# Experts in fp32 on unsplit weights, in groups of 32 slots over four column tiles, with empty groups left out on PE

## The chip, the cores and the metric

One core of a Trainium2 chip runs the whole program in one launch. The metric is the device time of one execution in microseconds. PE multiplies matrices, DVE, ACT and POOL work on vectors, SP issues loads; each runs its own queue of instructions in order. Products land in PSUM, a memory of eight banks of 128 partitions x 512 fp32 values.

## The reference

Two layers act on 256 latent and 256 context tokens of 1024 features. Layer 0 has a recurrent mixer (RG-LRU) and a dense SwiGLU, layer 1 has neighbourhood attention and, for the latent tokens alone, a mixture of eight experts. The change is in the experts:

```python
D_MODEL, SEQ, D_FF, N_EXPERTS, TOP_K = 1024, 256, 3584, 8, 2

def swiglu(z, w_gu, w_down):
    g, u = jnp.split(z @ w_gu, 2, axis=-1)
    return (jax.nn.silu(g) * u) @ w_down

def moe_swiglu(z, router, w_gu, w_down):
    logits = (z @ router).astype(jnp.float32)
    top_v, top_i = lax.top_k(logits, TOP_K)
    wts = jax.nn.softmax(top_v, axis=-1)
    gates = jnp.sum(jax.nn.one_hot(top_i, N_EXPERTS, dtype=jnp.float32) * wts[..., None], axis=-2)
    out = jnp.zeros_like(z)
    for e in range(N_EXPERTS):
        out = out + gates[..., e:e + 1].astype(z.dtype) * swiglu(z, w_gu[e], w_down[e])
    return out
```

All weights are fp32. The experts' are 8 x (1024 x 7168 + 3584 x 1024) values, 352 MB. On the reference's own inputs the router sends 19, 86, 51, 92, 45, 74, 37 and 108 of the 512 choices to experts 0 to 7.

## The kernel before

The program works through layer 0, attention, the output projection with the router, and then the experts, all on one core. Almost every product is made of float32r products: `mm3` (lines 297 to 301) splits both operands into a high and a low part and sums high x high, high x low and low x high, 128 x 128 stationary by up to 512 columns moving.

An expert's weights are cut into 1 MB tiles of 128 partitions x 2048 values: 28 tiles `m_up` (gate and up columns of 512 hidden features, four tiles for each of seven chunks) and 14 tiles `m_down` (two for each chunk), 336 tiles for eight experts. `plan2` lists them in the order of their use. The class `Halves` (lines 200 to 248) moves them. `load` (line 208) takes a free buffer and has SP issue the load (line 212) as long as there are free buffers. `split` (line 216) takes half of a tile: ACT copies it to the high part `whi` (line 224), and DVE, or every 13th time POOL, writes the rest `wlo` (line 229). After the second half the 1 MB buffer is free and the next load may start. `M.ahead` lets four halves be split ahead of their use. There are 17 buffers of 1 MB for the experts: five of their own (`NR`) and those that the weights of the earlier stages give back at the end of the output projection.

An expert has 128 slots. `onehots` (line 1291) compares a token's position in the expert with the slot numbers, `gather` (line 1300) multiplies the turned tokens by these and gives the expert's tokens `xghi`, `xglo`, features on partitions. `up_chunk` (line 1339) multiplies the tokens as stationary operand by the 512 gate and the 512 up columns of a chunk, 48 products, into the banks `pg` and `pu`; then silu, a product, and `turn` (line 1358), four transposes, whose result is split again. `down_chunk` (line 1373) adds 24 products to the two banks `py`. All 128 slots are computed, however many are filled: 72 products for a chunk, 4032 for the eight experts. `gated` (line 1416) scales by the gate, and `combine` (line 1425) brings the slots back to the tokens with the turned one-hots `oht` and adds to `xl`. The loop at line 1472 runs eight experts x seven chunks; a chunk's down products are behind the up products of the next chunk, and the gather of the next expert is at the end of chunk 6. Small steps stand between the up tiles (`between`). What follows a product on ACT or DVE is held in `late` and written behind the next split, so that the splits come first on these engines. The experts stand under a manual schedule: the order of the program is that of the code.

At the end (line 1516) each engine reads the largest number of an expert's tokens and branches past a loop (line 1517) that handles more than 128 tokens.

Of the kernel before, what the change touches and what calls it, by code (L numbers as in the profile page):

```python
# [35 lines left out]
NCOL = C_LT + 64  # L36

# The steps of the mixer in the order of the program: what, which tile, on which engines.
# [16 lines left out]
# The steps of a head in attention, and how many heads ahead of the values.  # L55
# [3 lines left out]
# Buffers, and how far the experts' splits run ahead: in general and in the last chunk and the last products.  # L59
NW, NH, NL = 7, 5, 5  # L60
AHEAD, AH6, AHL, THIRD = 4, 3, 2, 13
NU, NM, NR, LEAD = 45, 8, 5, 3
# [18 lines left out]
class Weights:  # L81
    """The weights in the order of their use: a load starts as soon as a buffer is free, splits run `split` tiles ahead."""
# [45 lines left out]
    def in_two(self, how=None, lazy=False):  # L128
        """The high part of the next tile; the low one with the call of what it returns."""
# [45 lines left out]
    def get(self, key):  # L175
        """The next tile; it is used up before the next call, if it isn't split."""
# [23 lines left out]
class Halves:  # L200
    """The experts' weights, split by half tiles, `ahead` of them ahead: a load starts as soon as a buffer is free."""

    def __init__(self, nc, free, plan, q, hi=None, lo=None, ahead=1):
        self.nc, self.free, self.plan, self.q, self.hi, self.lo, self.ahead = nc, list(free), plan, q, hi, lo, ahead
        self.i = self.dma = self.spl = self.third = 0
        self.t, self.parts = {}, {}
# [9 lines left out]
    def split(self):  # L216
        """The high part of the next half; the low one with the call of what it returns."""
        self.load()
        i, h = divmod(self.spl, 2)
        assert i < self.dma  # L220
        r, pool = self.t[i]
        s = r[:, h * D:(h + 1) * D]
        hi, lo = (p.tile([P, D], F32R, name=n, tag="w") for p, n in ((self.hi, "whi"), (self.lo, "wlo")))
        self.nc.scalar.activation(hi, s, AF.Copy)  # L224
        eng = self.nc.gpsimd if self.third and self.spl % self.third == 0 else self.nc.vector
        self.spl += 1

        def rest():
            eng.tensor_tensor(lo, s, hi.bitcast(F32), op=OP.subtract)  # L229
            self.parts[2 * i + h] = hi, lo  # L230
            if h:
                del self.t[i]
                self.free.append(pool)
                self.load()

        return rest

    def ready(self):
        while self.spl < min(self.i + self.ahead, 2 * len(self.plan)):
            self.split()()  # L240

    def get(self, key):
        assert self.plan[self.i // 2][0] == key
        self.i += 1
        self.ready()
        if self.spl < self.i:
            self.split()()
        return self.parts.pop(self.i - 1)


def build(tc, a, out):
# [5 lines left out]
    with tc.tile_pool(name="k", bufs=1) as kp, \  # L257
# [112 lines left out]
        for e in range(NE):  # L370
            for c in range(7):
                for i in range(4):
                    plan2.append(("mup", a["m_up"][e, 4 * c + i]))
                if e or c:
                    for i in range(2):
                        plan2.append(("mdown", a["m_down"][e if c else e - 1, 2 * ((c - 1) % 7) + i]))
        for i in range(2):
            plan2.append(("mdown", a["m_down"][NE - 1, 12 + i]))
        M = Halves(nc, [], plan2, nc.sync)
# [3 lines left out]
        # ---- constants and inputs  # L383
# [27 lines left out]
        def warm(n):  # L411
            """Products of zeros: the tensor engine's clock is up only after a while of work."""
# [8 lines left out]
        def ada_dve(raw, l, c, f, vs):  # L421
            """One tile of 128 columns of the modulation: a product and a sum over k."""
# [15 lines left out]
        # ---- RMS norms: sums of squares with the tokens on partitions, the factors turned back  # L438
        class Norm:
            """`vs` are the context's and the latent tokens (0 and 1) or one of the two."""  # L440
# [44 lines left out]
            def start(self, k, xk, vs=None):  # L485
                """h = x * rstd * A + B, as its float32r part and, with end, the rest."""
# [77 lines left out]
        # ---- layer 0: the first norm and its modulation, in two halves of the features  # L564
# [7 lines left out]
        def ada_first(k):  # L572
            """Shift and scale of 128 features, with a sum over four parts of k left."""
# [17 lines left out]
        # ---- RG-LRU: input branch, with k outside so that the products follow the modulation  # L591
# [43 lines left out]
        def two_parts(name, src, how):  # L635
            """The float32r part of a tile and the rest; `how` has the engines."""
# [12 lines left out]
        def do_in(f, how):  # L649
            """The last two tiles of the input branch."""  # L650
# [9 lines left out]
        def do_decay(n, how):  # L660
            """softplus(-lam) as max(-lam, 0) + log1p(exp(-|lam|)), the last by its atanh series."""
# [31 lines left out]
        def do_gz(f, how):  # L693
            """A tile of the gate branch."""
# [14 lines left out]
        def do_gate(i, how):  # L709
            """The two gates of a tile and a direction."""  # L710
# [18 lines left out]
        def do_coef(i, how):  # L729
            """a and 1 - a^2; 1 - a = -expm1(log a) = tanh(-log a / 2) (1 + exp(log a))."""  # L730
# [48 lines left out]
        def do_ada(i, how):  # L779
            """A tile of the modulations of the first residual and of the second norm; the last four have two rows of tiles."""  # L780
# [29 lines left out]
        def do_po(k, how):  # L810
            """What a tile of y adds to the first columns of the output projection."""
# [69 lines left out]
        # ---- SwiGLU of layer 0  # L881
# [71 lines left out]
        # ---- neighbourhood attention of layer 1: keys, queries and their norms  # L953
# [17 lines left out]
        def head_sums(f, x, ps, n):  # L971
            """The sums of squares of the tile's two heads, on the heads' partitions."""
# [74 lines left out]
        # ---- attention, a pipeline over the heads; queries on partitions in the scores  # L1047
# [141 lines left out]
        M.hi, M.lo = (stack.enter_context(tc.tile_pool(name=n, bufs=b)) for n, b in (("mhi", NH), ("mlo", NL)))  # L1189
        M.ahead, M.third = AHEAD, THIRD  # L1190
# [4 lines left out]
        # ---- output projection; the router and the turned tokens take x * A before the norm's factor and shift  # L1195
# [86 lines left out]
        def flush():  # L1282
            while late:
                late.pop(0)()
# [397 lines left out]
```

## Time and profile before

| | |
|---|---|
| median of two runs | 1972.46 us (1970.64 to 1974.28) |
| the profiled execution | span 1972.6 us |
| PE busy | 1912.1 us (97%) |
| DVE, ACT, POOL busy | 1548.6, 1204.5, 326.4 us |
| DMA, mean over the span | 250 GB/s |
| experts' tiles loaded | 336 of 1 MB |

A row of a group gives the line, the engine, the operation, what it writes and reads, how often it ran, its busy time and the mean of one. Ends of products are modelled from their starts, so products that follow each other overlap in the rows: the distance of two starts is what one costs. The 40 slices of the page are 49.3 us each.

### The profile page before, as it was taken

What the parts mean: (1) busy time and instruction counts of PE and PEld (TensorE: products, weight loads), DVE (VectorE), ACT (ScalarE), POOL (GpSimd) and SP (SyncE); (2) the same over time, 40 slices, a digit from 0 to 9 for tenths busy, and PEclk for the clock granted to TensorE, in tenths of its full rate; (3) what the DMA queues carried; (4) which work ended last, traced back from release to release, by engine and by line L of the source; (5) the groups of instructions that cost most, each with busy time, mean ns of one, the idle gap of its engine ahead of it and who ended that gap; (6) DMA issues with size and microseconds to landing.
All of it is one profiled execution on the core that took longest, in us unless ns stands there. A gap on an engine that the chain in (4) does not pass through costs nothing.

```text
span 1972.6 us, 25338 instructions
## 1 busy us (share of the span) xinstructions
PE 1912.1 (97%) x9467; PEld 1592.9 (81%) x9467; DVE 1548.6 (79%) x2023; ACT 1204.5 (61%) x1488; POOL 326.4 (17%) x218
## 2 busy tenths in 40 slices
PE   9995899999999999999999999999999999999998
PEld 7773688888888888878888888888888888888886
DVE  4799868767454663558798998999989999899997
ACT  4576443222222235457688788787887877878785
POOL 0277600000000012325011110101111011111110
PEclk8997899999999999999999999999999999999999
DMA  9462225435353552321899999999999999999990
GB/s 360 149 235 113 92 85 175 175 130 203 128 183 130 184 184 86 127 76 60 345 366 375 343 361 349 355 372 342 361 358 355 364 340 364 350 357 365 346 351 23
DMA packets 76019, 493.97 MB, mean 250 GB/s; under 512 B 8560, under 2 KB 9600, under 8 KB 20336
## 3 DMA queue, kind: packets, MB, share of 16 engines
q1 hardware_dynamic: 74592, 487.62, 66.4%
q0 software_dynamic: 1296, 4.65, 0.7%
q8 instruction: 76, 1.25, 0.3%
q14 instruction: 55, 0.45, 0.1%
HBM read 491.19 MB, written 1.05 MB: 250 GB/s over the span
## 4 chain that ended last, share of the span: by engine, by line
PE 54%; DVE 2%; issue 0%; ACT 0%; POOL 0%; DVEq 0%; POOLq 0%; ACTq 0%
PE pg L299 5%; PE py L299 5%; PE pg L301 5%; PE pu L299 5%; PE pg L300 5%; PE pu L301 5%; PE pu L300 5%; PE py L301 5%; PE py L300 5%; PE pgx L1305 2%; PE pt L1362 1%; PE ptt L1110 0%; PE po L299 0%; PE po L300 0%; PE po L301 0%; DVE ps L1086 0%
## 5 line engine op out<-in xcount | busy, mean ns | idle before, releaser
L229 DVE TENSOR_TENSOR wlo<-raw,whi 128x1024 fp32r<-128x1024 f32 x620 | 784.9, 1300 | 75.9 <-ACT whi L224 58.8
L224 ACT ACTIVATE whi<-raw 128x1024 fp32r<-128x1024 f32 x672 | 712.9, 1062 | 187.1 <-PE pu L301 136.6
L145 ACT ACTIVATE whi<-raw 128x2048 fp32r<-128x2048 f32 (+2 forms) x72 | 125.6, 1748 | 263.2 <-PE pu L300 116.5
L229 POOL TENSOR_TENSOR wlo<-raw,whi 128x1024 fp32r<-128x1024 f32 x52 | 130.0, 2500 | 885.9 <-ACT whi L224 849.2
L151 DVE TENSOR_TENSOR wlo<-raw,whi 128x2048 fp32r<-128x2048 f32 (+2 forms) x75 | 161.2, 2153 | 82.2 <-ACT whi L145 72.6
L299 PE MATMUL pg<-whi,xghi 128*128 128x512 f32 x448 | 179.3, 400 | 0.0
L299 PE MATMUL py<-whi,mhi 128*128 128x512 f32 x448 | 175.8, 392 | 0.0
L299 PE MATMUL pu<-whi,xghi 128*128 128x512 f32 x448 | 175.0, 391 | 0.0
L301 PE MATMUL pg<-whi,xglo 128*128 128x512 f32 x448 | 174.8, 390 | 0.0
L300 PE MATMUL pg<-wlo,xghi 128*128 128x512 f32 x448 | 174.8, 390 | 0.0
L301 PE MATMUL pu<-whi,xglo 128*128 128x512 f32 x448 | 174.6, 390 | 0.0
L300 PE MATMUL py<-wlo,mhi 128*128 128x512 f32 x448 | 174.5, 389 | 0.0
L301 PE MATMUL py<-whi,mlo 128*128 128x512 f32 x448 | 174.4, 389 | 0.0
L300 PE MATMUL pu<-wlo,xghi 128*128 128x512 f32 x448 | 174.4, 389 | 0.0
L301 PEld LDWEIGHTS pg<-whi,xglo 128*128 128x128 f32 x448 | 84.1, 188 | 18.2
L301 PEld LDWEIGHTS pu<-whi,xglo 128*128 128x128 f32 x448 | 84.1, 188 | 18.2
L300 PEld LDWEIGHTS pu<-wlo,xghi 128*128 128x128 f32 x448 | 84.1, 188 | 18.1
L299 PEld LDWEIGHTS pu<-whi,xghi 128*128 128x128 f32 x448 | 84.1, 188 | 18.1
L301 PEld LDWEIGHTS py<-whi,mlo 128*128 128x128 f32 x448 | 84.1, 188 | 17.7
L151 POOL TENSOR_TENSOR wlo<-raw,whi 128x2048 fp32r<-128x2048 f32 x4 | 18.9, 4717 | 478.3 <-ACT whi L145 478.2
L299 PEld LDWEIGHTS py<-whi,mhi 128*128 128x128 f32 x448 | 84.2, 188 | 16.7
L300 PEld LDWEIGHTS py<-wlo,mhi 128*128 128x128 f32 x448 | 84.2, 188 | 16.7
(340 smaller groups left out, 4077.1 us busy)
## 6 DMA issues: line engine op xcount, KB each, us to landing
raw<-m_up SPq DMA_DIRECT2D x224, 1024.0 KB, 6.8
raw<-m_down SPq DMA_DIRECT2D x112, 1024.0 KB, 6.9
raw<-w_up SPq DMA_DIRECT2D x28, 1024.0 KB, 4.8
raw<-ada SPq DMA_DIRECT2D x28, 1024.0 KB, 4.9
raw<-w_down SPq DMA_DIRECT2D x16, 896.0 KB, 4.6
raw<-ada0c SPq DMA_DIRECT2D x12, 1024.0 KB, 4.9
ada<-ada SPq DMA_DIRECT2D x32, 256.0 KB, 6.6
raw<-w_gz SPq DMA_DIRECT2D x4, 1024.0 KB, 8.3
```

Of the source, the lines that this page charges most:

```text
L145: self.nc.scalar.activation(hi[:, s], t[0][:, s], AF.Copy)
L151: eng.tensor_tensor(lo[:, s], t[0][:, s], hi[:, s].bitcast(F32), op=OP.subtract)
L224: self.nc.scalar.activation(hi, s, AF.Copy)
L229: eng.tensor_tensor(lo, s, hi.bitcast(F32), op=OP.subtract)
L299: mm(ps, lhsT=lh, rhs=rh, start=first, stop=False)
L300: mm(ps, lhsT=lh, rhs=rl, start=False, stop=False)
L301: mm(ps, lhsT=ll, rhs=rh, start=False, stop=last)
L1305: mm(ps[:, k * P:(k + 1) * P], lhsT=ht[q][h][:, k * P:(k + 1) * P], rhs=oh[:, T + q * P:T + (q + 1) * P], start=q == 0, stop=q == 1)
L1362: nc.tensor.transpose(ps[:, j * P:(j + 1) * P], s[:, j * P:(j + 1) * P], ident)
```

## The change

The experts no longer split anything: tokens, weights and hidden features are multiplied in fp32, one product where three stood. The class `Halves` becomes `Tiles`: `get` hands out a whole loaded tile, and `release` gives all tiles of a chunk back at its end, behind the last product that reads them. The experts have eight buffers of their own for loads, and 18 with those given back.

The 128 slots are four groups of 32 (`G`). A product takes 32 slots as stationary operand (128 x 32) and 256 columns; four products in turn go to the four column tiles of the array, each with its own 256 columns, and write 32 partitions of the same bank. Two banks hold four groups. Group 0 of a tile is multiplied as soon as the tile is there. Groups 1 to 3 of all tiles of a chunk stand at its end, in conditions on PE alone, nested in each other (`groups`): `n` is the number of groups beyond the first that are not empty, read by PE once for each expert. Banks are filled with zeros before, so that groups left out give zeros. The return to the tokens is in row tiles of 32 slots, and `way_back` makes the turned one-hots for each group.

```diff
+G = 32
+NG = P // G
...
+    def get(self, key):
+        r, pool = self.t.pop(self.i)
+        self.held.append(pool)
+        self.i += 1
+        return r
+    def release(self):
+        self.free += self.held
+        self.held = []
         self.load()
-        hi, lo = (p.tile([P, D], F32R, name=n, tag="w") for p, n in ((self.hi, "whi"), (self.lo, "wlo")))
-        self.nc.scalar.activation(hi, s, AF.Copy)
...
-            eng.tensor_tensor(lo, s, hi.bitcast(F32), op=OP.subtract)
...
-                    mm3(pg, g, [w[:, :512] for w in w2], k == 0, k == KT - 1)
-                    mm3(pu, g, [w[:, 512:] for w in w2], k == 0, k == KT - 1)
+        def up_jobs(ps, xg, w, i, g):
+            for k in (2 * i, 2 * i + 1):
+                for c in range(4):
+                    o = ((k % 2) * 4 + c) * T
+                    mm(ps[g // 2][G * c:G * (c + 1), (g % 2) * T:(g % 2 + 1) * T],
+                       lhsT=xg[k // 4][:, (k % 4) * P + g * G:(k % 4) * P + (g + 1) * G], rhs=w[:, o:o + T],
+                       start=k == 0 and g % 2 == 0, stop=k == KT - 1, tile_position=(0, G * c), skip_group_check=True)
+        def down_jobs(ps, m, w, c, i, g):
+            for j in (2 * i, 2 * i + 1):
+                for q in range(4):
+                    o = (j % 2) * D + q * T
+                    mm(ps[g // 2][G * q:G * (q + 1), (g % 2) * T:(g % 2 + 1) * T],
+                       lhsT=m[:, g * P + j * G:g * P + (j + 1) * G], rhs=w[:, o:o + T],
+                       start=c + j == 0 and g % 2 == 0, stop=(c, j) == (6, 3), tile_position=(0, G * q), skip_group_check=True)
+        def groups(n, *jobs):
+            def rest(g):
+                for job in jobs:
+                    job(g)
+                if g + 1 < NG:
+                    more(g + 1)
+            def more(g):
...
+                    with tc.If(n >= g):
+                        rest(g)
+            more(1)
...
+        def expert(tiles, xg, n, between, last=None):
+            for c in range(7):
+                ps = ahead.pop()
+                for i in range(4):
...
+                    ups.append(tiles.get("mup"))
+                    up_jobs(ps, xg, ups[i], i, 0)
+                    between(c, i)
+                    if i == 1 and c == 0 and last:
+                        last()
+                    if i == (2 if c == 1 else 1) and c:
+                        m = turn(s)
...
+                    for i in range(2):
+                        downs.append(tiles.get("mdown"))
+                        down_jobs(py, m, downs[i], c - 1, i, 0)
...
+                groups(n, *jobs)
+                tiles.release()
+                s = hidden(ps)
...
+            n = nc.tensor.value_load(ngi[0:1, e:e + 1], min_val=0, max_val=NG - 1)
```

On PE, in a chunk of an expert, before, the six products of one half of an up tile (`whi`, `wlo` are the weights' parts, `xghi`, `xglo` the tokens'; in brackets is what the row waits for):

```order
L299 MATMUL pg<-whi,xghi 128x512 [waits Activation_49]
L300 MATMUL pg<-wlo,xghi 128x512 [waits DVE_49]
L301 MATMUL pg<-whi,xglo 128x512
L299 MATMUL pu<-whi,xghi 128x512
L300 MATMUL pu<-wlo,xghi 128x512
L301 MATMUL pu<-whi,xglo 128x512
```

Each half tile waited for its two splits. On PE now, the end of such a chunk, from its last up tile (`raw` is the loaded tile, `xg` the tokens, `mt` the turned hidden features; `DMAHW` with a number is the completion count of a load):

```order
L1327 MATMUL pu<-raw,xg 32x256 [waits DMAHW3_49]
L1327 MATMUL pu<-raw,xg 32x256 x7
L1336 MATMUL py<-raw,mt 32x256 [waits DMAHW4_49,Activation_49]
L1336 MATMUL py<-raw,mt 32x256 x7
L1336 MATMUL py<-raw,mt 32x256 [waits DMAHW5_49]
L1336 MATMUL py<-raw,mt 32x256 x7
L1352 COMPARE_AND_BRANCH
L1327 MATMUL pu<-raw,xg 32x256 x32
L1336 MATMUL py<-raw,mt 32x256 x16
L1352 COMPARE_AND_BRANCH
L1327 MATMUL pu<-raw,xg 32x256 x32
L1336 MATMUL py<-raw,mt 32x256 x16
```

PE waits for the load itself, tile by tile; a third such group and the branches at the end follow. The conditions are on PE; the other engines have an unconditional branch in their place.

On SP the loads of the experts, before (L212), in the middle of an expert:

```order
L212 DMA raw<-m_up 128x2048 [waits DMAHW6_49,DVE_49]
L212 DMA raw<-m_up 128x2048 [waits DMAHW7_49,DVE_49]
L212 DMA raw<-m_up 128x2048 [waits DMAHW0_49,DVE_49]
L212 DMA raw<-m_up 128x2048 [waits DMAHW1_49,DVE_49,Pool_49]
L212 DMA raw<-m_down 128x2048 [waits DMAHW2_49,DVE_49]
```

and now (L214):

```order
L214 DMA raw<-m_up 128x2048 [waits DMAHW3_49,PE_49]
L214 DMA raw<-m_up 128x2048 [waits DMAHW4_49,PE_49]
L214 DMA raw<-m_up 128x2048 [waits DMAHW5_49,PE_49]
L214 DMA raw<-m_down 128x2048 [waits DMAHW6_49,PE_49]
L214 DMA raw<-m_down 128x2048 [waits DMAHW7_49,PE_49]
```

A load waited for the subtraction that freed its buffer, and now waits for the products that read it. In both, the eight completion counts are used in turn, and a load waits for the one eight before it.

## Rows read from the trace of the kernel before

**Rows 1.** The page's 40 slices: PE, DMA share (tenths), GB/s.
```profile
PE   9995899999999999999999999999999999999998
...
DMA  9462225435353552321899999999999999999990
GB/s 360 149 235 113 92 85 175 175 130 203 128 183 130 184 184 86 127 76 60 345 366 375 343 361 349 355 372 342 361 358 355 364 340 364 350 357 365 346 351 23
```

**Rows 2.** Busy time by stages of the experts, columns in the first line.
```profile
core 0: us, PE busy (x) PEld busy (x) DVE busy (x) ACT busy (x) POOL busy (x), PEclk, DMA share, GB/s
...
1000.00:1100.00 100.00, 100.00 (x475) 83.36 (x475) 89.31 (x90) 79.73 (x89) 12.00 (x5) 1.00 0.96 364
...
1700.00:1800.00 100.00, 100.00 (x479) 83.66 (x478) 90.78 (x97) 79.80 (x90) 12.13 (x5) 1.00 0.94 350
...
1900.00:1972.00 72.00, 64.88 (x297) 53.10 (x296) 57.73 (x58) 47.47 (x52) 7.26 (x3) 0.97 0.34 128
```

**Rows 3.** Waits from 900 on: us in total, times, longest.
```profile
ACT whi L224 <- PE pu L301: 136.6, 424, 0.9
...
SPq L212 <- DVE wlo L229: 757.8, 319, 11.9
```

**Rows 4.** The chain that ended last, two pieces: start, us, what.
```profile
1083.68 3.57 PE pgx L1305 x32
...
1207.63 3.57 PE pgx L1305 x32
```

**Rows 5.** The costliest groups: busy us, mean ns of one, idle before.
```profile
L229 DVE TENSOR_TENSOR wlo<-raw,whi 128x1024 fp32r<-128x1024 f32 x620 | 784.9, 1300 | 75.9 <-ACT whi L224 58.8
L224 ACT ACTIVATE whi<-raw 128x1024 fp32r<-128x1024 f32 x672 | 712.9, 1062 | 187.1 <-PE pu L301 136.6
```

**Rows 6.** PE's timeline: start, us from first start to last end, what.
```profile
21.74 1.94 PE L577 MATMUL ada<-ada,cz 128*32 128x256 f32 x16
...
40.52 1.07 PE L577 MATMUL ada<-ada,cz 128*32 128x256 f32 x16
```

**Rows 7.** All products of L577: ns of one, min/median/max, first and last start.
```profile
L577 PE MATMUL ada<-ada,cz x128: 379/379/637, 16.7 to 58.6; 128*32 128x256 f32 x128
```

**Rows 8.** The stretches of rows 6 in the table by stages, for the clock.
```profile
40.00:41.60 1.60, 1.60 (x20) 0.66 (x18) 0.00 (x0) 0.00 (x0) 0.00 (x0) 1.00 1.02 410
21.70:23.60 1.90, 1.90 (x17) 0.60 (x16) 1.71 (x4) 0.90 (x2) 0.00 (x0) 0.50 1.03 385
```

**Rows 9.** Line 1517, the branch at the end: ns min/median/max.
```profile
L1517 ACTq COMPARE_BRANCH  x1: 50/50/50, 1964.7 to 1964.7; - x1
L1517 PEldq COMPARE_BRANCH  x1: 4235/4235/4235, 1965.7 to 1965.7; - x1
```

**Rows 10.** Timelines of SP and PE: the loads from 935, the first expert product.
```profile
935.81 6.04 SPq L212 DMA_DIRECT2D raw<-m_up  x6
...
975.47 0.47 PE L299 MATMUL pg<-whi,xghi 128*128 128x512 f32 x1
```

**Rows 11.** The page's DMA issues: count, KB, us from issue to landing.
```profile
raw<-m_up SPq DMA_DIRECT2D x224, 1024.0 KB, 6.8
```

**Rows 12.** The table by stages where the experts' first loads run.
```profile
940.00:945.00 5.00, 5.00 (x46) 5.00 (x44) 4.18 (x4) 2.67 (x4) 0.00 (x0) 1.00 1.01 415
945.00:950.00 5.00, 5.00 (x45) 5.00 (x45) 3.00 (x7) 2.29 (x4) 0.00 (x0) 1.00 1.01 424
950.00:955.00 5.00, 5.00 (x45) 5.00 (x44) 4.59 (x2) 1.96 (x5) 2.87 (x1) 1.00 0.97 406
```

**Rows 13.** The table by stages around a pause of PE in layer 0.
```profile
182.00:192.00 10.00, 0.74 (x4) 0.27 (x2) 9.76 (x10) 6.59 (x9) 8.69 (x7) 0.66 0.30 105
192.00:202.00 10.00, 6.91 (x15) 4.96 (x16) 10.00 (x5) 6.90 (x11) 9.69 (x5) 0.50 0.00 0
202.00:206.00 4.00, 4.00 (x27) 3.61 (x26) 3.12 (x6) 3.93 (x5) 0.62 (x1) 0.97 0.00 0
```

**Rows 14.** The end, in the timeline: last sums, last four stores.
```profile
1964.96 1.67 DVE L1437 SCALAR_TENSOR_TENSOR xl<-pc,mod,xl 128x256 f32<-128x256 f32 x4
...
1965.46 1.80 SPq L1411 DMA_DIRECT2D out<-xl  x4
```

More of the change, by code (lines that the diff above doesn't have):

```diff
@@ L35 @@
 C_LT = 231
-NCOL = C_LT + 64
+C_SLOT = C_LT + 64
+NCOL = C_SLOT + 4
 MIXER = (
@@ L1511, in build @@
-        flush()
-        last_chunk(old)
-        assert W.i == len(plan) and M.i == 2 * len(plan2)
+                       rhs=oh[:, q * P:(q + 1) * P], start=q == 0, stop=q == 1)
+            xg = X("xg")
+            for k in range(4):
+                o, b = slice(k * P, (k + 1) * P), mod[:, 1, 3, 4 * h + k, 1:2]
+                if k % 2:
+                    act(xg[:, o], ps[:, o], AF.Identity, bias=b)
+                else:
+                    ts(xg[:, o], ps[:, o], b, None, op0=OP.add)
@@ new lines, in hidden, with turn @@
+        def hidden(ps):
+            s = U("ms")
+            for b in range(2):
+                o = s[:, b * T:(b + 1) * T].rearrange("p (g j) -> p g j", g=2)
+                gu = ps[b].rearrange("p (g h j) -> p g h j", g=2, h=2)
+                act(o, gu[:, :, 0], AF.Silu)
+                tt(o, o, gu[:, :, 1], op=OP.mult)
+            return s
+        def turn(s):
+            ps = PS("pt")
+            for g in range(NG):
+                nc.tensor.transpose(ps[:, g * P:(g + 1) * P], s[:, g * P:(g + 1) * P], ident)
+            m = U("mt")
+            act(m, ps, AF.Copy)
+            return m
@@ new lines, in gated @@
+        def gated(ps, back):
+            y = []
+            for b in range(2):
+                hi, lo = U("yhi", F32R), U("ylo", F32R)
+                for g in (2 * b, 2 * b + 1):
+                    o = slice((g % 2) * T, (g % 2 + 1) * T)
+                    act(hi[:, o], ps[b][:, o], AF.Copy, scale=back[1][:, g:g + 1])
+                    stt(lo[:, o], ps[b][:, o], back[1][:, g:g + 1], hi[:, o].bitcast(F32), op0=OP.mult, op1=OP.subtract)
+                y.append((hi, lo))
+            return y
@@ new lines, in last_part @@
+        def last_part(tiles, s, py, n, back):
+            m = turn(s)
+            downs = []
+            for i in range(2):
+                downs.append(tiles.get("mdown"))
+                down_jobs(py, m, downs[i], 6, i, 0)
+            groups(n, lambda g: [down_jobs(py, m, downs[i], 6, i, g) for i in range(2)])
+            return gated(py, back)
+        xg = [gather(onehots(pos[:, :, 0]), 0), None]
+        xg[1] = gather(onehots(pos[:, :, 0]), 1)
+        gates_and_most()
+        last, done = None, None
@@ new lines, in build, with between, last @@
+        for e in range(NE):
+            n = nc.tensor.value_load(ngi[0:1, e:e + 1], min_val=0, max_val=NG - 1)
+            back, xg2, oh = [], [], []
+            def between(c, i):
+                nonlocal done
+                if c == 1 and i == 1 and done:
+                    combine(*done)
+                    done = None
+                if c == 3 and i == 3:
+                    back.extend(way_back(pos[:, :, e], gates[:, :, e]))
+                if e + 1 < NE and c == 4 and i == 3:
+                    oh.append(onehots(pos[:, :, e + 1]))
+                if e + 1 < NE and c == 5 and i in (1, 3):
+                    xg2.append(gather(oh[0], i // 2))
+            s, py = expert(M, xg, n, between, last)
+            def last(s=s, py=py, n=n, back=back):
+                nonlocal done
+                done = last_part(M, s, py, n, back), back
+            xg = xg2
@@ L1516, in build @@
+        last()
+        M.release()
+        combine(*done)
+        for k in range(KT):
+            nc.sync.dma_start(out[:, k], xl[:, k])
+        assert W.i == len(plan) and M.i == len(plan2)
+        s = py = last = done = None
         n_most = nc.values_load(mosti[0:1, 0:1], min_val=0, max_val=T)
```

342 lines of the change are left out of this document (97 added, 245 removed).

## The prediction

> **What bounds the kernel now.** I read the page's 40 slices first. From slice 19 on PE reads 9 nearly everywhere, and DMA reads 9 with 340 to 375 GB/s [rows 1]: the experts are about half of the span, and two resources look full there at once. The table by stages says which one is. In each 100 us between 1000 and 1900 PE is busy for all 100 us at clock 1.00, while DMA is at about 0.95 and 350 to 364 GB/s [rows 2] (highest and lowest of nine such rows). So PE sets the pace. The waits agree: SP, which issues the weight loads, stands 757.8 us waiting for `wlo` of L229, and ACT's split waits 424 times for a product [rows 3]. Loads wait for splits to free a buffer, splits wait for products. A chunk (4 up tiles, 2 down tiles) is 72 products of 512 columns. Seven chunks and a gather take from one `pgx` (1083.68) to the next (1207.63), 123.95 us [rows 4]; 42 tiles of 1.0486 MB in that time are 355 GB/s. In the last stretch, 1900 to 1972, DMA is at 0.34 and PE at 64.88 of 72 us [rows 2]: the loads end near 1920 and PE works off its backlog.
>
> **What the change takes away.** The 620 subtractions of 1300 ns on DVE and the 672 copies of 1062 ns on ACT [rows 5] that split the experts' weights are gone (with POOL's 52), and with them the three products for one: 4032 products of 512 columns in 8 experts x 7 chunks. Neither DVE nor ACT was the limit, so their saving counts only in that a buffer no longer waits for them. The end moves by what PE loses.
>
> **What it adds on PE.** One group of 32 slots in one chunk is 32 up and 16 down products, 128x32 by 128x256 fp32, sent to four column tiles in turn. Before already runs this form: L577, four column tiles, each with its own moving operand. At clock 1.00 its 16 products last 1.07 us and one of them 0.38, so four rounds stand (1.07 - 0.38) / 3 = 0.23 us apart; at clock 0.50 it is (1.94 - 0.64) / 3 = 0.43 us [rows 6 to 8]. The four tiles do run side by side. A group in a chunk is 12 rounds: 2.8 us at 2.4 GHz, 5.2 us at 1.2 GHz. The reference's inputs send 19, 86, 51, 92, 45, 74, 37 and 108 tokens to the experts, so 1, 3, 2, 3, 2, 3, 2 and 4 groups are not empty: 20 in all, 20 x 7 x 12 = 1680 rounds, 386 us at the full clock and 720 us at half, against some 990 us of products now. Beside them a chunk has four transposes with an ACT copy (about 1 us) and the conditions.
>
> **What it adds as a condition.** Where a condition fails, PE branches past the remaining bodies, waits for its own count of finished products, and branches again. Before has one such jump past a long body on PE: 4235 ns; on ACT the branch itself reads 50 ns [rows 9]. So a failed condition, one in a chunk, is bounded by 0.05 and 4.2 us. I take 2 us, the middle; it is hidden wherever PE has slack. Expert 7 (four groups) fails none.
>
> **What bounds it then: the loads.** 334 of the 336 tiles are issued from 935.81 on [rows 10], as before; 334 x 1.0486 MB = 350.2 MB. SP now waits for PE's release of six tiles at a time, with 18 buffers and eight completion counts, so up to eight tiles are in flight. Before had two or three: 6.8 us to landing [rows 11], one issue per 2.9 us. How fast a deeper queue moves is shown where before had five or six in flight: 415, 424 and 406 GB/s from 940 to 955, with the DMA share at 0.97 to 1.01 [rows 12]. The lower bound is the stage's own 357 GB/s at 0.95, which is 375 at a full share. I take 415, the mean of the three rows, since the new queue is like them and not like the stage: 844 us. The bounds give 826 (424) and 934 (375).
>
> The Trainium skill speaks against this: "DMA: Bandwidth & Descriptors", section "Where 436 GB/s comes from", has the HBM side bind at about 358 GB/s per core. The trace exceeds it for 15 us [rows 12]; no row shows more for a whole stage. By that rule the loads would take 978 us.
>
> **What hides PE.** Six tiles at 415 GB/s arrive in 15.2 us. PE needs, with 1 us for the transposes and 2 us for the condition, 5.8, 8.6 and 11.4 us for one, two and three groups and 12.2 us for four at the full clock: hidden. At half clock it is 8.2, 13.4, 18.6 and 21.8 us: three and four groups stick out. Which clock it gets is open. In before a PE with 0.74 us of work between 182 and 192 stands at 0.50 until 202 and recovers after it has worked again [rows 13]; a PE that waits for tiles will see such stretches, and one that is late will see fewer. The ends are 0 and 21 x 3.4 + 7 x 6.6 = 118 us (77 with a condition for nothing). I take 15 us, because PE is late only where it is busy, and busy stretches stand at 1.00 [rows 2].
>
> **The sum.** 935.8 + 844 + 8 + 15 + 30 = **1833 us**. The 8 us: the 18 buffers are full by 976, and the first chunk, which starts where `pg` starts now, at 975.5 [rows 10], frees its tiles at about 984. The 30 us are the tail. The last two tiles land while PE is about 3 us from the end of chunk 6; then silu, transposes and copy 3, 16 rounds 3.7, four scalings and rests in turn 3, the combination's 64 products 2.5, eight sums of 0.42 us 3.4, and from the first of the last stores to the end 7.1 us (1965.46 to 1972.6) [rows 14]: 26 at the full clock, about 34 at half. The profiled execution is 1972.6 us and the median of the runs 1972.46, so nothing is corrected. DVE and ACT keep some 5 us of work in a chunk, of the sizes that they have now, behind 15.2 us of loads.
>
> **Rivals.**
> *The loads don't go faster.* The queue is deeper but the rate stays that of the stage. For it: 350 to 364 GB/s over 900 us [rows 2]. Against: the share is below 1 there, and an issue waits for a release. At 375 GB/s the end is at 935.8 + 934 + 8 + 30 = 1908 us; at 357, 1955.
> *PE binds in the long experts.* Half clock throughout, or a sequencer that needs as long for the 96 loads and products of a group (no row shows more than 16 such products in a run), makes the excess 77 to 118 us instead of 15: 1895 to 1936 us.
> *The conditions cost a long jump each (the other side).* At 4.2 us for each and half clock, three groups need 20.8 us a chunk, two 15.6, four 21.8: 21 x 5.6 + 21 x 0.4 + 7 x 6.6 = 172 us, so 1990 us. It turns slower than before by 2% (2012) from about 4.7 us each at half clock, and before's 4.2 us were seen with DMA nearly idle. Against: before's jump passes a whole loop, these at most three groups, and at the full clock PE has 3 us or more to spare.
> The Trainium skill, "Runtime: NRT & Kernel Launch", section "Instruction fetch mechanics", lets a taken branch out of the prefetched window wait for a fetch. The trace agrees with its 4235 ns [rows 9]; how long that is behind a full queue no row shows.
>
> **How the numbers follow.** As forecast (1795 to 1865) 0.56; under 1785 0.03; loads at about 375 0.12, at 357 0.08; PE in the long experts 0.12; the conditions 0.09, of which 0.05 over 2012. About 2% is what a measurement of this kernel can tell from no change, so faster means under 1933: 0.56 + 0.03 + 0.12 + 0.10 = 0.81; within 2%: 0.08 + 0.02 + 0.04 = 0.14; slower 0.05. From 1785 to 1940 lie the forecast, the loads at 375 and the long experts: 0.80.
>
> **What would show it.** Right: DMA share 1.0 and over 400 GB/s from 985 to 1790, PE's idle time ended by transfers, its rounds 0.23 or 0.43 us apart, SP hardly waiting. Wrong in the loads: DMA share 1.0 at 360 to 380 GB/s. Wrong in PE: DMA share falling in experts 1, 3, 5 and 7 at clock 0.5, and those experts longer than the others. Wrong in the conditions: branch rows of several us, and DMA idle also in experts with one or two groups.

## The result and the profile after

The changed kernel takes 2027.47 us (median of 2023.96 and 2030.98) against 1972.46 us before: a ratio of 1.028, 95% interval 1.022 to 1.033. It is slower by nearly 3%, where 1833 us was forecast. The profiled execution has a span of 2029.1 us.

The page's slices after, 50.7 us each, which answer to [rows 1]; PEclk is the granted clock in tenths:

```profile
PE   9996899999999999999768998789987899788997
...
PEclk9997899999999999999778998889988999988999
DMA  9352325344444533216898989779888888887740
GB/s 361 146 219 109 115 79 200 143 180 162 162 168 140 195 105 124 106 56 273 342 423 334 366 328 368 314 319 365 344 342 342 358 318 332 353 352 304 312 200 23
```

Up to slice 18 PE reads nearly as before. From 19 on, where PE read 9 nearly throughout, it now dips to 6, 7 and 8, its clock dips with it, and DMA moves no more than before, but for one slice at 423 GB/s. Neither PE nor DMA is full: something else holds both.

PE reads its count of groups once for each expert (`value_load`, at the head of the loop over experts), so the trace can be cut there: the eight experts start at 972.1, 1066.6, 1200.0, 1328.9, 1459.8, 1587.6, 1720.7 and 1849.4 us, and the last one's end is at 2016.4. The table by stages for the first three, the fourth and the last (1, 3, 2, 3 and 4 groups; columns in the first line, which answers to [rows 2]):

```profile
core 0: us, PE busy (x) PEld busy (x) DVE busy (x) ACT busy (x) POOL busy (x), PEclk, DMA share, GB/s
972.10:1066.60 94.50, 61.85 (x716) 33.93 (x714) 17.22 (x54) 9.63 (x24) 0.00 (x0) 0.78 0.92 380
1066.60:1200.00 133.40, 124.66 (x2080) 73.66 (x2080) 22.48 (x61) 13.21 (x31) 0.00 (x0) 0.95 0.84 339
1200.00:1328.90 128.90, 100.44 (x1504) 56.56 (x1504) 22.24 (x60) 12.83 (x30) 0.00 (x0) 0.89 0.86 345
1328.90:1459.80 130.90, 124.92 (x2112) 75.12 (x2112) 22.14 (x60) 12.65 (x30) 0.00 (x0) 0.96 0.85 339
1849.40:2016.40 167.00, 162.72 (x2908) 96.79 (x2908) 22.78 (x59) 13.93 (x31) 0.00 (x0) 0.98 0.51 203
```

Before, an expert took 123.95 us whatever its tokens [rows 4]. Now the one with one group takes 94.5, those with two 127.7 to 128.9, those with three 130.9 to 133.4, the one with four 167.0. Only the first is shorter. And an expert with two groups is hardly shorter than one with three, although PE is busy for 24 us less in it: 28 us of its stretch PE does nothing.

What PE waits for (waits of the whole span: us in total, times, longest), beside SP's wait for PE, which answers to [rows 3]:

```profile
ACT ms L1369 <- PEq L1352: 262.0, 48, 8.6
...
PE pu L1327 <- PEq L1352: 92.1, 45, 5.6
...
SPq L214 <- PEq L1352: 712.1, 49, 18.4
...
PE pu L1327 <- DMA raw<-m_up: 5.0, 1, 5.0
```

PE waits for a load once, 5.0 us. It waits 45 times for its own sequencer at line 1352, the conditions; ACT's silu stands behind them; and SP stands 712.1 us for PE to come past them and give the tiles back. So the loads are late because PE is late. The branch rows of line 1352 (ns min/median/max), in the first expert, in the second (three groups) and in the third (two groups):

```profile
L1352 PEldq COMPARE_BRANCH  x7: 3372/5946/6077, 976.0 to 1060.4; - x7
...
L1352 PEldq COMPARE_BRANCH  x29: 64/181/3332, 1076.0 to 1199.8; - x29
...
L1352 PEldq COMPARE_BRANCH  x25: 64/176/6527, 1206.0 to 1328.7; - x25
```

The branch of a condition that holds reads 64 ns. One that fails and passes three groups' products takes 5.9 to 6.1 us in six of seven chunks; one past two groups mostly 2 to 6.5 us; one past one group mostly 0.2 to 1.8 us, seldom 3. The rows of an expert add up to 39.1 us with one group, 30.6, 30.4 and 34.0 with two, 10.0, 8.7 and 10.4 with three, and 3.5 with four: 166.7 us.

One such pause, and the price of a group, in the timeline (start, us, what, and the idle time before):

```profile
1096.87 3.64 PE L1327 MATMUL pu<-raw,xg 128*32 128x256 f32 x64
...
1102.05 3.64 PE L1327 MATMUL pu<-raw,xg 128*32 128x256 f32 x64
...
1283.71 1.90 PE L1336 MATMUL py<-raw,mt 128*32 128x256 f32 x32
...
1290.83 0.38 ACT L1369 ACTIVATE ms<-pu 128x256 f32<-128x256 f32 x1 [6.50 <-PEq L1352]
...
1291.25 3.43 PE L1327 MATMUL pu<-raw,xg 128*32 128x256 f32 x32 [5.64 <-PEq L1352]
```

Group 3's products start 5.18 us after group 2's: that is a group in a chunk at the full clock. From 1285.6 to 1291.25 PE stands idle for the branch that began at 1284.16 and took 6.53 us. Behind the pause 32 records of a kind that lasts 1.9 us at the full clock take 3.43 us: the granted clock falls to its lower level, 1.2 GHz, as the table by stages shows behind the pause:

```profile
1284.00:1291.00 7.00, 1.61 (x32) 0.64 (x24) 0.42 (x1) 0.51 (x2) 0.00 (x0) 0.99 0.77 320
1291.00:1295.00 4.00, 3.75 (x35) 1.97 (x36) 0.42 (x1) 0.22 (x1) 0.00 (x0) 0.58 0.76 268
```

Over the experts the granted clock stands at 0.5 for 157 us.

### The profile page after: what moved, and what is told of

It reads as the page before. It is cut to its first block, busy times and chain, and to the rows that moved or that the text cites. A ratio compares the mean times of both kernels' runs of the same rounds, so it can differ in the third digit from the quotient of the medians.

```text
span 2029.1 us, 43145 instructions
## 1 busy us (share of the span) xinstructions
PE 1816.4 (90%) x19243; PEld 1290.2 (64%) x19243; DVE 818.5 (40%) x1593; ACT 513.8 (25%) x846; POOL 198.6 (10%) x166
## 5 line engine op out<-in xcount | busy, mean ns | idle before, releaser
L1327 PE MATMUL pu<-raw,xg 128*32 128x256 f32 x8960 | 571.7, 403 | 140.5 <-PEq L1352 92.1
L1327 PEld LDWEIGHTS pu<-raw,xg 128*32 128x32 f32 x8960 | 305.1, 115 | 368.2 <-issue 131.0
L1336 PE MATMUL py<-raw,mt 128*32 128x256 f32 x4480 | 270.9, 385 | 5.6 <-ACT mt L1378 5.6
L1336 PEld LDWEIGHTS py<-raw,mt 128*32 128x32 f32 x4480 | 143.2, 111 | 107.6 <-ACT mt L1378 9.5
L281 PE MATMUL pd<-flo,whi 128*128 128x512 f32 x210 | 81.8, 390 | 0.0
L282 PE MATMUL pd<-fhi,wlo 128*128 128x512 f32 x210 | 81.7, 389 | 0.0
L280 PE MATMUL pd<-fhi,whi 128*128 128x512 f32 x210 | 81.7, 389 | 0.0
L281 PE MATMUL pg<-hlo,whi 128*128 128x512 f32 x208 | 80.9, 389 | 0.0
L282 PE MATMUL pg<-hhi,wlo 128*128 128x512 f32 x208 | 80.9, 389 | 0.0
L280 PE MATMUL pg<-hhi,whi 128*128 128x512 f32 x208 | 80.9, 389 | 0.0
```

The lines of the kernel that those rows point to most:

```text
L280: mm(ps, lhsT=lh, rhs=rh, start=first, stop=False)
L281: mm(ps, lhsT=lh, rhs=rl, start=False, stop=False)
L282: mm(ps, lhsT=ll, rhs=rh, start=False, stop=last)
L1327: mm(ps[g // 2][G * c:G * (c + 1), (g % 2) * T:(g % 2 + 1) * T], lhsT=xg[k // 4][:, (k % 4) * P + g * G:(k % 4) * P + (g + 1) * G], rhs=w[ ...
L1336: mm(ps[g // 2][G * q:G * (q + 1), (g % 2) * T:(g % 2 + 1) * T], lhsT=m[:, g * P + j * G:g * P + (j + 1) * G], rhs=w[:, o:o + T], start=c ...
```

## The experiments

All are built from the changed kernel. An expert's time is the distance of two readings of its count; where no count is read, it is the distance of two `oht` rows of neighbouring experts (runs 3 and 4, where all experts are alike) or of their first up products (runs 1 and 11). Runs 3, 4, 6, 8, 10 and 11 were measured once.

**1. The counts written into the program.** The conditions are gone, the products that run are the same (for these inputs alone).

```diff
+                elif isinstance(n, int):
+                    if n >= g:
+                        rest(g)
...
-            n = nc.tensor.value_load(ngi[0:1, e:e + 1], min_val=0, max_val=NG - 1)
+            n = (0, 2, 1, 2, 1, 2, 1, 3)[e]
```

> The number of groups of each expert (1, 3, 2, 3, 2, 3, 2, 4 for these inputs) is written into the program, and the conditions are gone; the products that run are those of the changed kernel. Theory A (the conditions cost what the trace shows on TensorE's branches, 39 us in the first expert, 30 to 34 in each expert of two groups, 9 to 10 in each of three, 167 in all, and TensorE is the bound in all of them): about 1870 us, 1840 to 1900; an expert of three groups takes 125 us, one of two groups 95 to 100, and the granted clock stays over 0.95 in the experts. Rival B (the pauses at the conditions lie beside waits for weights that would be there anyway): 2000 to 2030 us, with TensorE waiting for the loads instead.

Measured: 1852.18 us, 0.938 of before (0.936 to 0.939). Two stages of its table (same columns):

```profile
1100.00:1200.00 100.00, 99.31 (x1771) 60.77 (x1767) 18.85 (x52) 11.59 (x28) 0.00 (x0) 1.00 1.01 424
1200.00:1300.00 100.00, 96.90 (x1664) 57.75 (x1660) 22.12 (x61) 12.16 (x30) 0.00 (x0) 0.98 1.01 425
```

PE and DMA are both full, at 424 GB/s. The conditions cost 2027 - 1852 = 175 us, the branch rows' 167 us and a little more; theory A stands. An expert takes 61 us with one group, 91 to 92 with two and 120 to 125 with three, and in the changed kernel, read in the same way, 94, 128 to 129 and 131 to 133: of the 175 us about 32 lie in the expert with one group, 111 in those with two and 33 in those with three. The granted clock is at 0.5 for 35 us of the experts instead of 157.

**2. Conditions one behind the other.** Each jump passes one group instead of up to three.

```diff
-                if g + 1 < NG:
-                    more(g + 1)
...
+            for g in range(1, NG):
...
                     with tc.If(n >= g):
-                        rest(g)
...
+                        for job in jobs:
+                            job(g)
```

> The conditions of a chunk stand one behind the other instead of nested, so that each jump passes one body, never two or three. Theory A (the price of a jump rises with the length of what it passes: 0.2 to 0.6 us past one body, 2 to 6.5 past two or three): the first expert loses 25 to 35 us of its branches and each of the three experts of two groups 20 to 25; about 1940 us, 1915 to 1970. Rival C (each jump that is taken costs the same few microseconds, whatever it passes): three jumps instead of one in the first expert and two instead of one in those of two groups; 2030 us or more, to 2150.

Measured: 2048.26 us, 1.038 (1.035 to 1.042), slower than the nested form. Neither theory fits: in the first expert the 21 branches read 218/2709/5824 ns (min/median/max). The first of a chunk's three took 0.2 to 0.8 us in six of seven chunks, the two behind it mostly 1.5 to 5.8. It is neither the length of one jump nor a fixed price; it matters what stands between two jumps.

**3. One group everywhere, no conditions.** Groups 2 to 4 are left out.

```diff
-            n = nc.tensor.value_load(ngi[0:1, e:e + 1], min_val=0, max_val=NG - 1)
+            n = 0
```

> Only the first 32 slots of each expert are computed, without conditions: the products of groups 2 to 4 are left out, the loads are all there. Theory A: TensorE needs some 55 us an expert, so the loads set the time: 1800 to 1830 us if they run at the 415 GB/s read before the experts, up to 1880 at the 376 GB/s of the changed kernel's first expert. Rival D (the loads, not TensorE, hold the changed kernel back): 1950 us or more.

Measured: 1789.68 us, 10 us under theory A's range. With PE busy for two thirds of the time the loads run at this rate throughout:

```profile
1100.00:1200.00 100.00, 68.17 (x784) 31.20 (x784) 20.22 (x56) 11.83 (x29) 0.00 (x0) 0.82 1.01 426
```

An expert takes 104 us. This is the floor that the loads set; rival D falls.

**4. Four groups everywhere, no conditions.**

```diff
-            n = nc.tensor.value_load(ngi[0:1, e:e + 1], min_val=0, max_val=NG - 1)
+            n = 3
```

> All four groups of every expert, without conditions; nothing is left out. Theory A (a group costs 5.2 us in a chunk, 0.43 us for a round of four column tiles): every expert takes about 160 us as the last one does, together 972 + 8 x 160 + 12 = 2265 us, 2240 to 2300. Rival E (the step as it was predicted, 0.23 us for a round and 2.8 us for a group): TensorE would need 3.45 + 4 x 2.8 us less one up part, near 100 us an expert, and the loads would set the time: under 2000 us.

Measured: 2248.35 us; every expert takes 157.8 us, so the price of a group is 5.2 us in a chunk, and rival E, the prediction's own 2.8 us, falls. The trace of this run also shows how much code PE reads; over 600 us without a jump (the table by stages, and the DMA queues in the same stretch: packets, MB, share):

```profile
1200.00:1800.00 600.00, 597.25 (x10724) 362.94 (x10716) 83.84 (x224) 49.32 (x112) 0.00 (x0) 1.00 0.69 279
```

```profile
q8 instruction: 84, 1.38, 0.9%
```

84 packets of 16,384 bytes for 21,440 rows of PE and PEld are 64 bytes a row. A product of this form has four rows, so a group's 48 products in a chunk are 12.3 KB of code, two are 24.6, three are 36.9, and a packet holds 1.3 groups.

That pointed to code. In the changed kernel 37 of the 208 branches of line 1352 took over 1 us, and every one of the 37 ends 1.35 to 1.54 us after the end of such a packet. Of the 171 shorter ones, three hold the end of a packet. The packet itself lasts 0.9 to 1.4 us; in the median pause it starts 1.5 us after the branch, in the longest 4.2 us after. So a long pause is a wait for a packet of code. That it is the code at the jump's target is the likely reading; the trace shows no addresses.

**5. Shorter jumps in more places.** The condition stands behind each two up tiles and behind the down tiles, 16 products a group instead of 48.

```diff
+                    if i % 2:
+                        groups(n, lambda g: [up_jobs(ps, xg, ups[j], j, g) for j in (i - 1, i)])
-                jobs = [lambda g: [up_jobs(ps, xg, ups[i], i, g) for i in range(4)]]
+                jobs = []
```

> Conditions of a chunk in three places: after each two tiles of the up projection (16 products a group) and after the down projection (16 a group), instead of one place behind all of them (48 a group). What is passed in a chunk is the same in sum, but no jump passes more than 48 products, and the common work of the chunk stands between the jumps. Theory G (a jump is cheap, 0.2 to 0.6 us, while what it jumps to has been fetched, and costs a fetch of 16 KB of TensorE's code, 3 to 6 us, when it reaches beyond; the common work between the jumps lets the fetches catch up): 21 x 0.3 to 0.5 us an expert, together 50 to 85 us on the 1852 us without conditions, some of it beside waits for loads: 1890 to 1930 us. Rival C (every taken jump costs a fetch of its own): 21 jumps of 3 to 6 us in seven of the experts, 2150 us or more.

Measured: 2063.21 us, 1.046 (1.044 to 1.048). Both theories missed. The first expert's 20 branches read 317/3922/5124 ns and add up to 71.5 us: each jump passes 12.3 KB, and the 16 common products between two jumps last 1.7 us, less than half of the median pause. In the experts with three groups, where a jump passes 4 KB and 5 us lie between, the failing ones take 0.2 to 0.35 us nearly always.

**6. No loads behind the first 18** (the tiles are used again and again, so the weights are wrong; 318 loads are left out).

```diff
+            if isinstance(pool, tuple):
+                r, pool = pool
+            else:
...
-        self.held.append(pool)
+        self.held.append((r, pool))
```

> The conditions as in the changed kernel, but the experts' first 18 tiles of weights are used again and again, so that the other 318 loads are left out (the sums are of wrong weights). Theory H (a jump's pause is the fetch of code, and most of it is the fetch standing behind weight loads in the DMA engines): the taken jumps of the first expert fall from 5.9 us to under 3.5 us each, the branches' sum of the experts from 167 us to 80 to 100, and the whole to 1900 to 1950 us. Rival F (the price of a jump doesn't depend on the loads): branches 150 to 175 us, whole 2000 us or more.

Measured: 1923.07 us. The branches of its first expert, with DMA at a share of 0.05:

```profile
L1355 PEldq COMPARE_BRANCH  x7: 3372/3795/4192, 978.1 to 1043.3; - x7
```

3.8 us instead of 5.9, and 105 us in the sum over the experts instead of 167. Rival F falls, and theory H holds in its direction, not in its "most of it" (the branches' sum is just above its 80 to 100). A third of the pause goes with the loads, and two thirds remain when nothing is loaded. The packets show where the third lies: in the first expert they start 0.9 to 1.5 us after the branch here, and 3.4 to 3.7 us after it in six of seven chunks of the changed kernel, while the packet itself is no shorter.

**7. and 8. Two groups always, conditions apart or behind.** Groups 1 and 2 without a condition; in 7, group 3 behind the third up tile, its rest and group 4 behind the down tiles, so that 5.2 us of common products stand ahead of each jump; in 8, both nested at the end of the chunk. In 7 the loads are in another order too, the two down tiles ahead of the fourth up tile; 8 keeps the old order.

```diff
+            elif first:
+                with tc.If(n >= 2):
+                    third()
+            else:
+                with tc.If(n >= 2):
+                    up(3, 2)
+                    with tc.If(n >= 3):
+                        fourth()
...
+                    for g in (0, 1):
+                        up_jobs(ps, xg, ups[i], i, g)
```

> Groups 1 and 2 are always computed (the first expert then has two instead of one); group 3 stands under a condition after the third tile of the up projection, its rest and group 4 under another after the down projection. Each jump passes one body of 40 to 56 products, with about 5.2 us of common products ahead of it. Theory G (a jump past about one body, with some 5 us of products ahead of it in which the code is fetched, costs 0.2 to 0.6 us; only jumps past two or three bodies, or close behind another jump, cost a fetch): branches of 5 to 8 us in each expert instead of 30 to 39; 1885 to 1925 us, faster than both kernels. Rival C (every jump that is taken costs a fetch of 2 to 6 us): two of them in 7 chunks of four experts, 2060 us or more.

> The same products as in the run with two groups always, but the two conditions nested behind all common work of the chunk, as the changed kernel has them; a jump of an expert of two groups passes 96 products. Theory G: the four experts of two groups take about 128 us each, as three do in the changed kernel; 2040 to 2075 us. If the length of what is passed doesn't matter (rival C): one jump a chunk instead of the other run's two, and so faster than that run.

Measured: 2035.17 us for 7 (1.030; 1.0285 to 1.032) and 2045.76 for 8. Run 8 is as expected, run 7 missed by over 100 us. Its two conditions, in the third expert:

```profile
L1382 PEldq COMPARE_BRANCH  x7: 218/353/2426, 1232.6 to 1334.7; - x7
...
L1385 PEldq COMPARE_BRANCH  x7: 334/1301/5816, 1234.7 to 1345.1; - x7
```

Most jumps of the one are cheap, half of the other's are not. A chunk is 49 KB of code, three packets, for 10.4 us of products, and the pauses of run 6's first expert are 3.4 us or more for one packet even without loads: three such fetches would take as long as the work. So the theory was changed once more: what counts is how much code, run or passed, comes to how much work.

**9. and 10. The two common groups as one of 64 slots.** Two column tiles of 64 slots instead of four of 32: the same rounds with half the instructions, and the way back to the tokens to match. 9 has the conditions and the loads as in 7, 10 as in 8.

```diff
+        def up_wide(ps, xg, w, i):
+            for k in (2 * i, 2 * i + 1):
+                for c in range(4):
+                    o = ((k % 2) * 4 + c) * T
+                    b = 2 * G * (c % 2)
+                    mm(ps[0][b:b + 2 * G, (c // 2) * T:(c // 2 + 1) * T],
+                       lhsT=xg[k // 4][:, (k % 4) * P:(k % 4) * P + 2 * G], rhs=w[:, o:o + T],
...
```

> As the run with two groups always and the conditions apart, but these two groups are computed together in two column tiles of 64 slots instead of twice four of 32: the same rounds of TensorE with half the instructions, 48 products a chunk instead of 96, so that a chunk's code falls by a quarter. Theory G2 (the pauses are fetches of code, and what sets their sum is how much code, run or passed, has to be fetched beside how much work): the chunk of an expert of two groups has 37 KB of code instead of 49 for its 10.4 us; branches of 6 to 14 us in such an expert instead of 22 to 30, 1885 to 1935 us in all, faster than both kernels. Rival I (the pause belongs to the jump, not to the amount of code): the same 22 to 30 us of branches and 2015 to 2045 us.

> The same 64-slot products, with the two conditions nested behind the common work of the chunk; a jump of an expert of two groups passes 96 products at once. Theory G2: one jump past more than a fetch's 16 KB pauses 2 to 4 us in each chunk of the four experts of two groups; 1915 to 1990 us, slower than with the conditions apart. Rival I: 2030 to 2050 us, as the run with 32-slot products.

Measured: 1973.27 us for 9, 0.9999 of before (0.998 to 1.0015), and 2003.94 for 10. The branches of an expert with two groups fall to 12.9 to 14.7 us in 9, from 21.6 to 30.5 in 7, and the whole by 62 us; in 10 they are 24 to 34, nearly as in 8, and the whole falls by 42 us. For 9 that is about what theory G2 says of the branches, and rival I falls. For 10 theory G2 had 2 to 4 us a chunk, 14 to 28 us in an expert: with a quarter less code in the chunk than in 8 only a little went from the branches of these experts, and that part of the theory isn't borne out. Both times lie above their forecasts, by 38 and 14 us.

**11. The same without conditions.** Run 9 with the counts written in, and 2 groups for the first expert (the cut is against run 9).

```diff
-                with tc.If(n >= 2):
+                if n >= 2:
                     third()
...
-            n = nc.tensor.value_load(ngi[0:1, e:e + 1], min_val=0, max_val=NG - 1)
+            n = (0, 2, 1, 2, 1, 2, 1, 3)[e]
```

> The run with 64-slot products and conditions apart (1973 us, its branches 75 us in sum), with the numbers of groups written into the program and no conditions. If its remaining distance to the 1852 us of the first run without conditions is the branches: 1880 to 1910 us. If the 64-slot products are dearer than two times 32 slots, or the always computed second group of the first expert costs its 36 us in full: 1930 us or more.

Measured: 1867.28 us. So the wide form and the first expert's second group cost 15 us, and the conditions still 106 us, of which the branch rows show 75. An expert of two groups takes 88 us here and 107 to 111 in 9, one of three 124 and 132, the first 78 and 94: some 65 of the 106 us lie in the three experts of two groups.

**12. Two conditions instead of three.** Group 3 whole behind the up tiles, group 4 whole behind the down tiles, the loads in the changed kernel's order and not in that of run 9.

```diff
+                one(n, ps, xg, ups, py, m, downs, c, 2)
+                for j in range(len(downs)):
+                    down_wide(py, m, downs[j], c - 1, j)
+                one(n, ps, xg, ups, py, m, downs, c, 3)
```

> 64-slot products, and two conditions a chunk instead of three: group 3 whole behind the up projection, group 4 whole behind the down projection, 48 products each, with 6.9 and 3.5 us of common products ahead. Against the run with three conditions: 0.25 us less in each chunk of the experts of three and four groups (about 7 us in all); but if 3.5 us are too short for a fetch (a packet and what stands around it took some 4 us or more), a pause of 1 to 3 us in the chunks of the four experts of two groups, 28 to 84 us. 1965 us in the first case, 1995 to 2055 in the second; I expect about 1990.

Measured: 1942.82 us, 0.9845 of before (0.982 to 0.987), with the counts still read on the chip. It is the lowest time of the runs that keep the conditions and all loads, 85 us under the changed kernel. Against before it is 1.5% less: the interval is clear of 1, but the difference is inside the 2% that counts as no change here. Its second and third expert:

```profile
1067.60:1196.00 128.40, 123.36 (x1424) 78.98 (x1424) 21.17 (x57) 12.60 (x30) 0.00 (x0) 1.00 0.88 360
1196.00:1300.10 104.10, 91.21 (x816) 62.52 (x816) 21.32 (x57) 12.69 (x30) 0.00 (x0) 0.98 0.96 394
```

The expert with two groups has come down to 104 us, as long as one takes in run 3 at the loads' own pace. My 1990 was wrong: the pauses came as feared (its 14 failing branches in that expert read 207/1975/3861 ns), and the time fell all the same. Those with three groups take 126.7 to 128.4 us instead of 131.7. About half of that is seen at the end of a chunk (a chunk near 1141 us in both): PE idles 0.31 us there instead of 0.64, where one condition ends and not two nested ones. Why those with two groups gain 3 to 7 us on run 9, with more pauses, isn't settled; the places of the conditions and the order of the loads changed together with their number.

## Why the prediction was wrong

*What bound the kernel before*, and what goes from it, was read rightly; DVE and ACT fell to 818.5 and 513.8 us.

*The loads.* Right. With PE out of the way the tiles run at 426 GB/s (run 3), and at 410 to 426 in run 1, about the 415 taken from [rows 12]. The Trainium skill, "DMA: Bandwidth & Descriptors", section "Where 436 GB/s comes from", which would have had 978 us for them, doesn't hold here: run 1 reads at 410 to 426 GB/s for 15 slices of the page, 46 us each. But in the changed kernel the loads never came to bind: PE waited for one once, 5.0 us.

*A round of four column tiles.* Mis-sized, by a factor of nearly two. The step took the 16 records of L577 in [rows 6] for 16 products, four rounds. They are 8 products: the program has 64 on that line and the trace 128 rows [rows 7], as it has 8960 rows after on L1327 for 20 x 7 x 32 = 4480 products. Two rounds, not four: a round is 0.43 us at the full clock and 0.86 at half, a group in a chunk 5.2 us and not 2.8, the 1680 rounds 725 us and not 386. This alone didn't break the forecast. Run 1, with these rounds and no conditions, is at 1852 us, within the 1795 to 1865 given for the likeliest case. That is partly luck: its last tile lands at 1788 us, 15 us before the sum has it (all terms but the tail are 1803), and its tail is 33 us longer than forecast. But the dearer round ate the slack: three groups need 17 us of PE in a chunk for 15 us of loads, and the sum put the conditions' price behind that slack.

*The conditions.* The step that decided it: "I take 2 us, the middle; it is hidden wherever PE has slack". A chunk's failing conditions cost 5.6 us with one group (39.1 / 7), 4.5 with two (95.0 / 21) and 1.4 with three (29.1 / 21), and with PE as the bound nearly all of it is on the path: 175 us in run 1's difference. Nor could the loads hide it: the tiles are given back behind the conditions, so SP stood there with PE (712.1 us), and over the experts DMA moved 323 GB/s at a share of 0.80. The 4235 ns of [rows 9] was not the upper end: it was seen with DMA nearly idle, and past three groups run 6 shows 3.8 us without loads and the changed kernel 5.9 with them. The rival with long jumps had the mechanism, and got 0.09 of the chances. That its 172 us come so near the 175 is luck: it put 118 of them into the experts with three groups, 8 into those with two and 46 into the one with four, which fails no condition; run 1 finds 33 and 111 in the first two, and 32 in the expert with one group, for which the rival had nothing. It also stood on an end of 1818 us where 1852 was due. For the Trainium skill, "Runtime: NRT & Kernel Launch", section "Instruction fetch mechanics" (a taken branch out of the window of two 16 KB pages waits for a fetch), the trace now agrees: packets of 16,384 bytes, 0.2 to 1.8 us mostly for a jump past 12.3 KB with 15 us of products ahead of it, 2 to 6.5 us past 24.6 KB.

*The clock.* The 15 us stood for PE being late at half clock; the experts spend 157 us at 0.5 with the conditions and 35 without them (run 1). PE's work alone, from run 4's 157.8 us less 36.3 for each group missing, is 49 + 3 x 121.5 + 3 x 85.3 + 157.8 = 827 us; the changed kernel took 1044 (972.1 to 2016.4). Of the 217 us between them PE is idle for 146 (the branch rows' 167 us begin while products still run, as at 1284.16), and for the other 71 it is busy, 898 us in all. It was busy for 130 of the 157 us at 0.5; by half of these, an estimate from these rows, the clock accounts for 65 of the 71.

*The tail.* 30 us, forecast for a PE that waits for its last tiles. It was 63 us (the last load landed at 1965.8) and as much in run 1, as the last expert has four groups and PE is behind; where PE waits for loads, in run 3, it is 19.

## What to carry to other kernels

A runtime condition that skips work was priced here by the code it passes and the work ahead of it, not by its own 64 ns: count the bytes of instructions in a skipped body against a fetch of 16 KB, and the work ahead of the jump against the fetch's 4 to 6 us. If the engine that branches is the bound, make the code smaller first (half the instructions for the common groups saved 62 us here; two conditions instead of three, at other places, 30 more). Computing a part always, so that no jump is long, paid only together with the smaller code: alone it was 2035 us against 2027 (run 7). And before a duration is taken from a group of records, count the products in the program: a row isn't an instruction of the source.

## What the runs showed of the hardware

- An fp32 product of 128x32 by 128x256 leaves two weight loads and two products in the trace; a round of four column tiles costs 0.43 us at the full clock, and a round of two column tiles of 64 slots the same (3.67 us for 32 records, that is eight rounds of two, against 1.91 us for four rounds of four).
- PE's code is read at 64 bytes a row, in packets of 16,384 bytes; a pause for such a packet ends 1.35 to 1.54 us after it. Past 36.9 KB a pause is 3.4 to 4.2 us with DMA at a share of 0.05 (run 6), and 5.9 to 6.1 at 0.92, but for the first chunk.
- A jump past 12.3 KB with 15 us of products ahead of it mostly costs 0.2 to 1.8 us; with 1.7 us ahead it is 3.9 us in the median (run 5).
- Loads of 1 MB run at 410 to 426 GB/s through 15 slices of run 1 with up to eight in flight; before, with two or three in flight, it was 350 to 364 [rows 2, 11].
